# Stick-breaking weights from a scan of one product, its value halves added at the branch, and four more gate columns in a 7-product unit

## The chip, the cores and the metric

The kernel runs on one core of a Trainium2 chip. The metric is the device time of one execution in microseconds. The engines are TensorE (PE, with PEld for its weight loads), VectorE (DVE), ScalarE (ACT), GpSimd (POOL) and SyncE (SP), each with an instruction stream of its own; data moves between memory and the on-chip buffer by DMA, issued from SP and POOL.

## What is computed

One block of a transformer on 1024 tokens of width 1024, in float32: a norm and an input projection, three branches (stick-breaking attention with 8 heads of 64, forgetting attention with 8 heads of 64, attention of 4 heads of 128 over 256 memory tokens), each multiplied by a gate of 1024 columns and by a matrix of its own, their sum through an output matrix, and a squared-ReLU MLP. The change touches the stick-breaking branch and the gates:

```python
def stick_breaking_attention(q, k, v):
    """A[t,s] = beta[t,s] * prod_{s<j<t}(1-beta[t,j]), strictly causal."""
    ...
        z = jnp.einsum('bhtd,bhsd->bhts', q[:, :, q0:kend], k[:, :, :kend]) * scale
        log_rem = jnp.where(strict, jax.nn.log_sigmoid(-z), 0.0)
        after = lax.cumsum(log_rem, axis=3, reverse=True) - log_rem
        w = jnp.where(strict, jnp.exp(jax.nn.log_sigmoid(z) + after), 0.0)
        outs.append(jnp.einsum('bhts,bhsd->bhtd', w, v[:, :, :kend]))
```

With beta = sigmoid(z) and rho = 1 - beta, the weight of token s is what is left of a stick behind s, less what is left at s: A[s] = L[s+1] - L[s], where L[s] is the product of rho over s, s+1, ... up to the query.

## The kernel before

**Precision.** A float32 product is made of fp32r products (a form that TensorE multiplies at full rate): each operand is split into a high and a low part, high by ScalarE (L1054), low by VectorE as the difference (L1055), and three products are summed. A *7-product unit* is a scheme for a group of four column blocks of 128 of the input projection, in which operand sums save some products: 168 matmuls of 512 columns (or as many in pairs of 256) where four plain blocks take 4 x 48 = 192. The units are sbk, sbq, mq, fxk, fxq, sbv, ga, gb, gc, in this order (`PROJ`), the last three for the gates 16 to 19, 20 to 23 and 0 to 3 (`GATES`). The remaining gates are plain blocks (L1144).

**The order of the work.** The kernel is written as many small processes in Python that run when the program is built. Each asks a planner for operations (`Op(engine, estimated time, function, due)`), for buffers (`Get(pool)`) and for events. The planner keeps a clock per engine and takes the earliest due ready operation; a dense product is a side task, taken on TensorE only when no other TensorE operation is ready at that moment of its plan. What comes out is a fixed instruction order per engine; at run time nothing is reordered, and an engine waits at the head of its stream. Dense products are taken in one order (`dense`, L1107): values, one gate, the 7-product units, the plain gates, then the memory branch, the stick-breaking branch and, after attention, the forgetting branch.

**Attention.** `units` (L976) starts a `unit` (L887) per pair of heads, head and group of 256 queries, first the four stick-breaking pairs, then the four forgetting pairs. A unit has two tiles of 128 queries (`sb_tile` L812, `fox_tile` L851). For stick-breaking a chunk of up to 512 scores is made by two matmuls (L823, L824) into a PSUM bank; on the diagonal block VectorE adds the mask (L834); ScalarE makes two sigmoids, rho and beta (L827, L828); VectorE scans backwards (L843), c[s] = rho[s] c[s+1] + beta[s], in which c is what has been taken. The values were differenced once (`value_step` L1566) so that the product with c gives the sum over A. Then per block of 256 keys: four transposes on TensorE (*turn*, L917) into one of two TR banks, the high part by ScalarE (L922), the low part by VectorE (L924, `ptl`), four matmuls with the values (L934). At the end of a unit the result stands in PSUM as two halves of 64 rows, which ScalarE and VectorE add (L962, L963) before SP stores it to `o_scr`. Forgetting attention stores its two halves to `o_scr` and `low_scr`, and they are added when the branch fetches them (L1666, L1668). Memory attention (L627 on, normalised at L662) runs beside the last stick-breaking pairs.

**Buffers and the branches.** Three tiles of 1024 columns named `r` (pool `RR`) carry what the branches fetch; two of them are used as four half tiles for rho (`RQ`) until the stick-breaking pairs are over. `fetched_o` (L1658) loads a row block of 128 rows of a branch's attention result, `bring` (L1680) splits it into high and low parts for the matmul, and `dense_branch` (L1732) multiplies: the blocks ks[0], ks[1] first for both halves, then ks[2], ks[3]. For the stick-breaking branch, ks[2] and ks[3] are split into buffers that the memory branch reads until it is done.

## Time and profile before

| | |
|---|---|
| runs | 1685.86 us median of 3, 1685.47 to 1686.56 |
| the profiled execution | span 1686.7 us, 0.8 above that median |
| TensorE | 1675.3 us busy (99%), 9118 matmuls |
| VectorE | 1293.0 us (77%) |
| ScalarE | 848.9 us (50%) |
| POOL | 255.2 us (15%) |
| stick-breaking scores | from 483 to 703 us |
| forgetting scores | from 706 to 862 us |
| stick-breaking branch | 883 to 927 us |

The profile follows one execution. A row of the timeline is start, duration, engine, line, operation, output and inputs by the program's names, and in brackets how long the engine stood idle before it and what it waited for. A row of grouped instructions ends in the count, the busy time, the mean of one in ns, and the idle time before them. Matmuls overlap, so that their price is the distance between two starts. The granted clock is TensorE's clock as a share of the full one.

### The profile page before, as it was taken

To read this page: it belongs to the slowest core of one execution; us is meant where nothing else is said; L and a number is where in the kernel's file an instruction comes from. 1 tells how busy PE (TensorE), PEld (TensorE's weight loads), DVE (VectorE), ACT (ScalarE), POOL (GpSimd) and SP (SyncE) were. 2 spreads that over 40 slices of the span, in tenths; PEclk is the share of its full clock that TensorE was granted. 3 is DMA by queue.
4 is the path that set the end of the run, shared out by engine and by line. 5 is a ranking of instruction groups with operands and counts; after the bars stand their busy time and mean duration, and the time that the engine had idled before them with its cause. 6 is when DMAs were issued, how large, how long until landed. Compare 5 with 4: busy or idle time off the path is not lost.

```text
span 1686.7 us, 25003 instructions
## 1 busy us (share of the span) xinstructions
PE 1675.3 (99%) x9118; PEld 1432.0 (85%) x9118; DVE 1293.0 (77%) x2079; ACT 848.9 (50%) x1474; POOL 255.2 (15%) x440
## 2 busy tenths in 40 slices
PE   9999999999999999999999999999999999999999
PEld 9998899998888888888888887878888887888887
DVE  7977778855459888867877898987777776688775
ACT  6455555534358888866761446433333344332331
POOL 0000000000253151254400011022111120000000
PEclk9999999999999999999999999999999999999999
DMA  7445434467475365387747542144444484564532
GB/s 245 157 150 182 149 119 150 146 194 243 127 232 161 111 186 151 117 240 224 236 146 245 183 162 100 57 162 155 152 150 137 150 307 171 202 202 143 198 125 75
DMA packets 142221, 284.32 MB, mean 169 GB/s; under 512 B 16913, under 2 KB 53329, under 8 KB 142098
## 3 DMA queue, kind: packets, MB, share of 16 engines
q1 hardware_dynamic: 110562, 183.08, 32.0%
q0 software_dynamic: 31536, 99.64, 19.5%
q8 instruction: 72, 1.18, 0.3%
q14 instruction: 51, 0.42, 0.1%
HBM read 189.83 MB, written 92.83 MB: 168 GB/s over the span
## 4 chain that ended last, share of the span: by engine, by line
PE 92%; DVE 5%; DMA 2%; ACT 1%; issue 1%; SPq 0%; DVEq 0%; ACTq 0%
PE pp L1456 11%; PE pp L1144 10%; PE pp L1981 10%; PE pp L2658 8%; PE sc L1456 7%; PE sc L1144 6%; PE sc L1981 5%; PE sc L2658 4%; PE tr L2658 4%; PE tr L917 4%; PE pv L1456 3%; PE pv L2658 3%; PE tr L1981 2%; PE sc L934 2%; PE pp L934 2%; DVE h L1917 1%
## 5 line engine op out<-in xcount | busy, mean ns | idle before, releaser
L1055 DVE TENSOR_TENSOR wlo<-raw,whi 128x1024 fp32r<-128x1024 f32 (+1 forms) x88 | 107.5, 1222 | 80.2 <-ACT whi L1054 80.0
L1054 ACT ACTIVATE whi<-raw 128x1024 fp32r<-128x1024 f32 (+1 forms) x88 | 93.2, 1059 | 78.8 <-PE pp L1456 32.7
L2658 PE MATMUL pp<-h,sop 128*128 128x512 f32 x540 | 128.4, 396 | 0.0
L2658 PEld LDWEIGHTS pp<-h,sop 128*128 128x128 f32 x540 | 101.6, 188 | 24.4
L1981 PE MATMUL pp<-h,oh 128*128 128x512 f32 x384 | 121.1, 397 | 0.7 <-ACT cu L2066 0.6
L924 DVE TENSOR_TENSOR ptl<-tr,pth 128x512 fp32r<-128x512 f32 (+1 forms) x160 | 99.1, 628 | 24.1 <-ACT pth L922 23.1
L922 ACT ACTIVATE pth<-tr 128x512 fp32r<-128x512 f32 (+1 forms) x160 | 87.4, 556 | 36.0 <-PE sc L934 15.8
L1981 PEld LDWEIGHTS pp<-h,oh 128*128 128x128 f32 x384 | 72.0, 188 | 19.0 <-ACT cu L2066 1.4
L2573 ACT ACTIVATE h<-t 128x2048 fp32r<-128x2048 f32 (+1 forms) x17 | 30.7, 1814 | 110.2 <-DVE t L1917 97.4
L1373 POOL DMA_DIRECT2D raw<-w_in x32 | 24.2, 755 | 395.1 <-DVE wlo L1055 395.1
L1144 PE MATMUL sc<-h,whi 128*128 128x512 f32 (+1 forms) x254 | 77.7, 389 | 0.0
L1456 PE MATMUL pp<-h,whi 128*128 128x512 f32 x248 | 77.5, 394 | 0.0
L1981 PE MATMUL pp<-h,ol 128*128 128x512 f32 x192 | 76.1, 396 | 0.0
L1456 PE MATMUL pp<-whi,h 128*128 128x256 f32 x384 | 71.8, 283 | 0.0
L843 DVE TENSOR_TENSOR_SCAN e<-r,e 128x384 f32<-128x384 f32 (+3 forms) x64 | 66.3, 1044 | 6.9 <-ACT e L828 6.5
L1974 ACT ACTIVATE oh<-raw 128x512 fp32r<-128x512 f32 x64 | 39.4, 625 | 61.8 <-DVE raw L1917 61.8
L2658 PE MATMUL sc<-h,sop 128*128 128x512 f32 x264 | 63.7, 396 | 0.0
L2658 PE MATMUL tr<-h,sop 128*128 128x512 f32 x264 | 63.4, 396 | 0.0
L1917 DVE TENSOR_TENSOR sop<-ur,sop 128x2048 fp32r<-128x2048 f32 (+1 forms) x28 | 61.8, 2211 | 2.0 <-ACT sop L2586 2.0
L917 PE MATMUL tr<-ident,e 128*128 128x128 f32 x416 | 62.7, 273 | 0.0
L1456 PEld LDWEIGHTS pp<-whi,h 128*128 128x128 f32 x384 | 60.2, 188 | 0.0
L2658 PEld LDWEIGHTS sc<-h,sop 128*128 128x128 f32 x264 | 49.6, 188 | 12.3 <-DVE sop L1917 0.5
(558 smaller groups left out, 5087.7 us busy)
## 6 DMA issues: line engine op xcount, KB each, us to landing
ur<-s_scr SPq DMA_DIRECT2D x26, 1024.0 KB
raw<-w_in POOLq DMA_DIRECT2D x42, 512.0 KB, 4.9
raw<-w_up SPq DMA_DIRECT2D x60, 256.0 KB
s_scr<-s POOLq DMA_DIRECT2D x60, 256.0 KB, 2.7
g<-w_down SPq DMA_DIRECT2D x14, 1024.0 KB
s_scr<-cu POOLq DMA_DIRECT2D x48, 256.0 KB, 2.8
h<-sbk_scr POOLq DMA_DIRECT2D x64, 128.0 KB, 3.2
o<-gate_scr SPq DMA_DIRECT2D x32, 256.0 KB
```

Of the source, the lines that this page charges most:

```text
L843: nc.vector.tensor_tensor_scan(out=back, data0=rho[:, :u][:, ::-1], data1=back, initial=0.0 if last else beta[:, c + u:c + u + 1], op0=ALU ...
L917: nc.tensor.transpose(tr[:, jj * 256 + a * P:jj * 256 + (a + 1) * P], es[a][:, j * P:(j + 1) * P], ident)
L922: yield Op("ACT", act_time(512 - lo_c), lambda: nc.scalar.activation(ph[:, lo_c:], tr[:, lo_c:], AF.Copy))
L924: yield Op("DVE", dve_time(512 - lo_c), lambda: nc.vector.tensor_tensor(pl[:, lo_c:], tr[:, lo_c:], f32(ph[:, lo_c:]), ALU.subtract))
L934: nc.tensor.matmul(pv[0][:, c_:256], pair.v[:, j, b, :], p_[:, jj * 256 + c_:(jj + 1) * 256], start=(k == 0 and n_ == 0 and i == 0), stop= ...
L1054: yield Op("ACT", 0.03 + act_time(m), lambda: nc.scalar.activation(hi, raw, AF.Copy))
L1055: yield Op("DVE", dve_time(m), lambda: nc.vector.tensor_tensor(lo, raw, f32(hi), ALU.subtract))
L1144: nc.tensor.matmul(ps, a_, b_, start=(first and i == 0), stop=(last and i == n - 1))
L1456: nc.tensor.matmul(out_, a_, b_, start=(first and n == 0 and j == 0), stop=(last and n == 3 and j == len(todo) - 1), skip_group_check=True)
L1917: nc.vector.tensor_tensor(out_, a_, b_, op)
L1981: nc.tensor.matmul(ps, w[a_][:, k * P:(k + 1) * P], h[b_][k], start=(first and k == 0 and i == 0), stop=(last and k == 3 and i == 2), skip ...
L2658: nc.tensor.matmul(ps, a_[:, c, qs], b_[:, c, :], start=(kind in ("P1", "P2", "P7") and c == 0 and i == 0), stop=(kind in ("P2", "P4", "P3 ...
```

## The change

- **The scan.** L[s] = rho[s] L[s+1], from 1: the scan multiplies by rho and adds a zero. One sigmoid per score; beta, the second buffer for it and the pool `RQ` go, and the three `r` tiles are free from the start.
- **The mask.** In place of VectorE's add on the scores, POOL sets the masked entries of rho to 1 (`affine_select` on the diagonal 128 x 128 block), between the sigmoid and the scan.
- **The values** are differenced with the other sign, and 1 is subtracted from L as the blocks are read back from PSUM: ScalarE's copy gets a bias of -1 from a column `minus`, VectorE's subtraction becomes one instruction that adds -1 and subtracts the high part.
- **The halves.** A stick-breaking unit stores both halves as they are, as a forgetting unit does (`low_scr` becomes two). The branch fetches both for each row block, into two `r` tiles, and VectorE adds them.
- **The gates** 4 to 7 become a fourth gate unit `gd` of 7 products, after gc. Six plain gates stay (10 to 15), where there were ten.

```diff
-    def sb_tile(pair, b, i, beta):
+    def sb_tile(pair, b, i, left):
...
         def chunk(ci, c, m, u):
-            rho = yield Get(RQ)
             sc = yield Get(SC)
+            part = left[:, c:c + u]
...
-            def sigmoids():
-                nc.scalar.activation(rho[:, :u], sc[:, :u], AF.Sigmoid, scale=HD ** -0.5)
-                nc.scalar.activation(beta[:, c:c + u], sc[:, :u], AF.Sigmoid, scale=-HD ** -0.5)
-
             yield Op("PE", 2 * mm_time(max(m, 256)), scores)
+            yield Op("ACT", act_time(u), lambda: nc.scalar.activation(
+                part, sc[:, :u], AF.Sigmoid, scale=HD ** -0.5), table=AF.Sigmoid)
+            SC.put(sc)
             last = c + u == n
             if last:
-                dg = sc[:, u - P:u]
-                yield Op("DVE", 0.22, lambda: nc.vector.tensor_tensor(
-                    dg, dg, holder["later"][:, 385:513], ALU.add))
-            yield Op("ACT", act_time(u, u), sigmoids, table=AF.Sigmoid)
-            SC.put(sc)
-            if not last:
+                dg = left[:, n - P:n]
+                yield Op("POOL", 0.3, lambda: nc.gpsimd.affine_select(
+                    out=dg, in_=dg, pattern=[[-1, P]], compare_op=ALU.is_ge, fill=1.0, base=-1, channel_multiplier=1))
+            else:
                 yield scanned
-
-            def scan():
-                back = beta[:, c:c + u][:, ::-1]
-                nc.vector.tensor_tensor_scan(out=back, data0=rho[:, :u][:, ::-1], data1=back,
-                                             initial=0.0 if last else beta[:, c + u:c + u + 1],
-                                             op0=ALU.mult, op1=ALU.add)
-            yield Op("DVE", 0.1 + 0.00215 * u, scan, 0.14)
-            RQ.put(rho)
+            back = part[:, ::-1]
+            yield Op("DVE", 0.1 + 0.00215 * u, lambda: nc.vector.tensor_tensor_scan(
+                out=back, data0=back, data1=zero.to_broadcast([P, u]),
+                initial=1.0 if last else left[:, c + u:c + u + 1], op0=ALU.mult, op1=ALU.add), 0.14)
...
-            yield Op("ACT", act_time(512 - lo_c), lambda: nc.scalar.activation(ph[:, lo_c:], tr[:, lo_c:], AF.Copy))
+            h_, t_ = ph[:, lo_c:], tr[:, lo_c:]
+            yield Op("ACT", act_time(512 - lo_c), lambda: nc.scalar.activation(
+                h_, t_, AF.Identity, bias=minus) if of_sb else nc.scalar.activation(h_, t_, AF.Copy))
             pl = yield Get(PL)
-            yield Op("DVE", dve_time(512 - lo_c), lambda: nc.vector.tensor_tensor(
-                pl[:, lo_c:], tr[:, lo_c:], f32(ph[:, lo_c:]), ALU.subtract))
+            yield Op("DVE", dve_time(512 - lo_c), lambda: nc.vector.scalar_tensor_tensor(
+                pl[:, lo_c:], t_, -1.0, f32(h_), ALU.add, ALU.subtract) if of_sb else nc.vector.tensor_tensor(
+                pl[:, lo_c:], t_, f32(h_), ALU.subtract))
...
-        if pair.kind == "fox":
...
-        else:
-            o = ob[:HD, :]
-            yield Op("ACT", act_time(256), lambda: nc.scalar.activation(o, pv[0][HD:P, :256], AF.Copy))
-            yield Op("DVE", dve_time(256), lambda: nc.vector.tensor_tensor(o, o, pv[0][0:HD, :256], ALU.add))
-            PV.put(pv[0])
-            yield Op("SP", 0.1, lambda: nc.sync.dma_start(scr[rows, cols], o), 2.5)
+        yield Op("ACT", act_time(256), lambda: nc.scalar.activation(ob, pv[0][:, :256], AF.Copy))
+        PV.put(pv[0])
+
+        def halves():
+            nc.sync.dma_start(scr[rows, cols], ob[:HD, :])
+            nc.sync.dma_start(low[rows, cols], ob[HD:, :])
+        yield Op("SP", 0.2, halves, 3.0)
...
-    GATES = {"ga": 16, "gb": 20, "gc": 0}
+    GATES = {"ga": 16, "gb": 20, "gc": 0, "gd": 4}
...
-        yield Op("DVE", dve_time(512), lambda: nc.vector.tensor_tensor(a, a, b, ALU.subtract))
+        yield Op("DVE", dve_time(512), lambda: nc.vector.tensor_tensor(a, b, a, ALU.subtract))
...
-        halves = [RR.free.popleft() for _ in range(2)]
-        RQ.put(*(t[:, i * 512:(i + 1) * 512] for t in halves for i in range(2)))
-        spawn(whole_again(halves))
...
     def fetched_o(bi, k):
 
-        raw_ = yield Get(RR)
+        raw_, *low_ = (yield Get(RR, 2)) if bi == 1 else [(yield Get(RR))]
         raw, rows = raw_[:, :S], slice(k * P, (k + 1) * P)
         yield from transfer(lambda: nc.sync.dma_start(raw, o_scr[order[bi][1]][rows, :]), P * S * 4)
+        if bi == 1:
+            t = low_[0]
+            yield from transfer(lambda: nc.sync.dma_start(t, low_scr[0][rows, :]), P * S * 4)
+            yield Op("DVE", dve_time(S), lambda: nc.vector.tensor_tensor(raw, raw, t, ALU.add))
+            RR.put(t)
         if bi == 2:
             t = yield Get(RR)
-            yield from transfer(lambda: nc.sync.dma_start(t, low_scr[rows, :]), P * S * 4)
+            yield from transfer(lambda: nc.sync.dma_start(t, low_scr[1][rows, :]), P * S * 4)
```

Since the planner sets the order, the change moves instructions on every engine. In the pieces below the lines are those of the program they come from: the dense product is L1144 before and L1134 after, a turn L917 and L911, a product with values L934 and L931, the scores of stick-breaking L823, L824 and L824, L825. `g` and `h` are tiles of tokens or of attention results, `whi`/`wlo` high and low parts of weights, `pth`/`ptl` the two parts of a turned block, `e`/`es` rows of weights before they are turned, `sc`, `pp`, `pv`, `tr` PSUM banks.

First TensorE late in stick-breaking, with a plain gate between the pieces of attention, before:

```order
L934 MATMUL sc_137<-ptl_4802,v_4689 128x256
L1144 MATMUL pp_134<-g_122,whi_167 128x512
L1144 MATMUL pp_134<-g_126,whi_167 128x512
L1144 MATMUL pp_134<-g_122,wlo_168 128x512
L823 MATMUL pp_133<-h_4684,h_4682 128x512
L824 MATMUL pp_133<-h_4686,h_4682 128x512
L1144 MATMUL pp_134<-g_123,whi_167 128x512
L1144 MATMUL pp_134<-g_127,whi_167 128x512
L1144 MATMUL pp_134<-g_123,wlo_168 128x512
L934 MATMUL sc_137<-pth_4799,v_4689 128x256
```

And after, at the end of the last plain gate:

```order
L1134 MATMUL sc_139<-g_125,whi_169 128x512
L1134 MATMUL sc_139<-g_129,whi_169 128x512
L1134 MATMUL sc_139<-g_125,wlo_170 128x512
L824 MATMUL sc_138<-h_4899,h_4907 128x384
L825 MATMUL sc_138<-h_4905,h_4907 128x384
L911 MATMUL tr_140<-ident,e_4912 128x128
L911 MATMUL tr_140<-ident,e_4913 128x128
L911 MATMUL tr_140<-ident,e_4912 128x128
L911 MATMUL tr_140<-ident,e_4913 128x128
L931 MATMUL pp_137<-pth_5018,v_4908 128x256
L931 MATMUL pp_137<-ptl_5020,v_4908 128x256
```

Behind this point the next dense matmul stands 593 rows further on, the first of the memory branch; between them are attention and memory attention alone.

VectorE beside it after, a little into that piece (L920 is the low part of a stick-breaking block, L838 the scan, L661 and L663 the normalisation of memory attention):

```order
L920 SCALAR_TENSOR_TENSOR ptl_5020<-tr_140,pth_5018 128x512
L920 SCALAR_TENSOR_TENSOR ptl_5021<-tr_141,pth_5019 128x384
L661 RECIPROCAL st_6531<-st_6531 128x4
L663 TENSOR_SCALAR r_4914<-r_4914,st_6531 128x256 x4
L838 SCALAR_TENSOR_TENSOR e_4910<-e_4910,sm 128x384
L920 SCALAR_TENSOR_TENSOR ptl_5020<-tr_140,pth_5018 128x512
L920 SCALAR_TENSOR_TENSOR ptl_5021<-tr_141,pth_5019 128x512
L838 SCALAR_TENSOR_TENSOR e_4910<-e_4910,sm 128x512
L838 SCALAR_TENSOR_TENSOR e_4911<-e_4911,sm 128x512
```

No mask add stands between them any more, and the scan reads one row of weights in place of two.

Next VectorE between the memory branch and the stick-breaking branch, before (L1779 and L1781 evict results of a branch, L1055 is the low part of a split):

```order
L1779 TENSOR_TENSOR g_7469<-pp_134,o_4811 128x512
L1055 TENSOR_TENSOR wlo_164<-r_4694,whi_163 128x512
L1055 TENSOR_TENSOR h_7212<-r_4695,h_7212 128x512
L1055 TENSOR_TENSOR h_7213<-r_4696,h_7213 128x512
L1055 TENSOR_TENSOR wlo_164<-r_4694,whi_163 128x512
L1055 TENSOR_TENSOR h_7212<-r_4695,h_7212 128x512
L1055 TENSOR_TENSOR h_7213<-r_4696,h_7213 128x512
```

And after (L1649 adds the halves of a stick-breaking block, L1655 those of a forgetting block, L1766 and L1768 evict, L1045 is the low part of a split):

```order
L1649 TENSOR_TENSOR r_4914<-r_4914,r_4915 128x1024
L613 RECIPROCAL fn<-fn 128x16
L1766 TENSOR_TENSOR g_6608<-sc_139,o_5030 128x512
L1045 TENSOR_TENSOR wlo_168<-r_4914,whi_167 128x512
L1045 TENSOR_TENSOR h_6344<-r_4916,h_6344 128x512
L1045 TENSOR_TENSOR wlo_168<-r_4914,whi_167 128x512
L1045 TENSOR_TENSOR h_6344<-r_4916,h_6344 128x512
L1045 TENSOR_TENSOR wlo_170<-raw_171,whi_169 128x1024
L1649 TENSOR_TENSOR r_4915<-r_4915,r_4914 128x1024
L1045 TENSOR_TENSOR h_6343<-r_4915,h_6343 128x512 x2
L1655 TENSOR_TENSOR r_4916<-r_4916,e_4911 128x1024
```

Three tiles that held three fetched blocks now hold one block with its low half, and the next block's low half goes into the tile that the first leaves. SP's queue there, after (L1645 loads `o_scr`, L1648 the low half of a stick-breaking block, L1653 that of a forgetting block):

```order
L1645 DMA r_4915<-o_scr_75 128x1024
L1645 DMA r_4916<-o_scr_76 128x1024
L1645 DMA e_4910<-o_scr_76 128x1024
L1648 DMA r_4914<-low_scr_78 128x1024
L1653 DMA e_4911<-low_scr_79 128x1024
```

The low half of the last stick-breaking block stands behind two loads of the forgetting branch. TensorE's matmuls of that branch, after:

```order
L1134 MATMUL pp_135<-whi_167,whi_165 128x512
L1134 MATMUL pp_135<-wlo_168,whi_165 128x512
L1134 MATMUL pp_135<-whi_167,wlo_166 128x512
L1134 MATMUL pp_135<-h_6343,whi_165 128x512 x2
L1134 MATMUL pp_135<-h_6343,wlo_166 128x512
```

`h_6343` is the last block, reached after 15 matmuls of the branch.

26 lines of the change are left out of this document (9 added, 17 removed).

## Prediction

> **What bounds the kernel now.** I read first the page's engine totals and the shares of its chain:
>
> ```profile
> span 1686.7 us, 25003 instructions
> PE 1675.3 (99%) x9118; PEld 1432.0 (85%) x9118; DVE 1293.0 (77%) x2079; ACT 848.9 (50%) x1474; POOL 255.2 (15%) x440
> PE 92%; DVE 5%; DMA 2%; ACT 1%; issue 1%; SPq 0%; DVEq 0%; ACTq 0%
> ```
>
> TensorE is busy 99% of the span and holds 92% of the chain. So the time is the sum of its matmuls plus the moments in which it has none. An edit to VectorE, ScalarE or POOL counts only where TensorE waits for them. Next, the windows by stage (columns: stretch, length, PE, PEld, DVE, ACT, POOL busy, granted clock, DMA share, GB/s): dense products before attention, stick-breaking, forgetting attention, the second branch's product.
>
> ```profile
> 60.00:489.00 429.00, 428.77 (x2746) 387.99 (x2745) 296.47 (x494) 205.99 (x320) 43.80 (x68) 1.00 0.52 164
> 489.00:708.00 219.00, 219.00 (x1364) 193.29 (x1364) 191.16 (x343) 188.84 (x420) 68.53 (x123) 1.00 0.54 158
> 708.00:882.00 174.00, 172.53 (x1101) 152.17 (x1100) 133.65 (x358) 122.42 (x278) 63.51 (x117) 0.99 0.67 201
> 882.00:927.00 45.00, 45.00 (x197) 36.46 (x196) 35.02 (x48) 8.87 (x12) 2.24 (x3) 1.00 0.76 244
> ```
>
> In the stick-breaking stage TensorE is busy for 219.00 of 219.00 us although VectorE works 191 and ScalarE 189: dense gate matmuls between the attention matmuls keep it fed. The only place in attention where it runs dry is at 740, found in the list of waits and then on the timelines and windows:
>
> ```profile
> 731.58 0.33 SPq L1663 DMA_DIRECT2D r<-o_scr  x1
> 740.50 0.63 ACT L1054 ACTIVATE h<-r 128x512 fp32r<-128x512 f32 x1 [3.58 <-DMA r<-o_scr]
> 742.59 0.50 PE L869 MATMUL pv<-h,h 128*128 128x512 f32 x1 [1.47 <-DVE st L874]
> 740.33:743.75 3.42, 1.95 (x9) 1.14 (x8) 2.58 (x9) 3.04 (x6) 0.00 (x0) 1.00 0.96 322
> 743.75:747.16 3.41, 3.41 (x10) 2.61 (x9) 1.22 (x8) 2.05 (x4) 0.00 (x0) 0.50 0.99 342
> 1023.60:1027.00 3.40, 1.86 (x14) 1.59 (x14) 3.26 (x9) 3.33 (x6) 0.00 (x0) 1.00 0.94 280
> ```
>
> A 512 KB load took 8.9 us from issue to its reader (731.58 to 740.50), TensorE stood 1.47 us, and the next 3.41 us ran at a granted clock of 0.50, which loses about 1.7 us more. A like shortfall at 1023.60 shows 1.00 in its own window.
>
> **Matmuls.** Gates 4 to 7 took 4 x 48 = 192 matmuls of 512 columns; as a fourth 7-product unit they take 168.
>
> ```profile
> 160.82 5.57 PE pp L1456 x24
> 784.84 0.62 PE L917 MATMUL tr<-ident,e 128*128 128x128 f32 x4
> 785.22 0.42 PE L869 MATMUL pv<-h,h 128*128 128x384 f32 x1
> 785.48 0.34 PE L870 MATMUL pv<-h,h 68*128 68x384 f32 x1
> 785.65 0.28 PE L934 MATMUL pp<-pth,v 128*128 128x256 f32 x1
> 785.77 0.28 PE L934 MATMUL pp<-ptl,v 128*128 128x256 f32 x1
> ```
>
> 24 in 5.57 us is 0.232 each; 24 fewer save 5.6 us. The scores, turns and products stay. The unit's operand sums, splits and evictions lie in the stage 60 to 489, where VectorE has 132 us free and ScalarE 223: taken at nothing; without that cover they would cost their own time. Start to start, 128 columns cost 0.095 (four turns, 784.84 to 785.22), 256 cost 0.12, 384 cost 0.17.
>
> **The stretch without dense work.** With six dense gates left instead of ten, their matmuls run out in the order before stick-breaking ends. From the last of them to the first matmul of the memory branch there now stand 96 matmuls of 512 columns, 20 of 384, 226 of 256 and 287 of 128, attention and memory attention alone: 22.3 + 3.4 + 27.1 + 27.3 = 80 us of TensorE with nothing to fill it. The longest such piece before was about 5 us, and in it lies the stall at 740. What VectorE has to do beside those 80 us, by the rows of before:
>
> ```profile
> L843 DVE TENSOR_TENSOR_SCAN e<-r,e 128x512 f32<-128x512 f32 x40 | 50.4, 1264 | 3.5 <-ACT e L828 3.1
> L843 DVE TENSOR_TENSOR_SCAN e<-r,e 128x384 f32<-128x384 f32 x8 | 7.5, 943 | 1.9 <-ACT e L828 1.9
> L924 DVE TENSOR_TENSOR ptl<-tr,pth 128x512 fp32r<-128x512 f32 x96 | 65.1, 682 | 18.4 <-ACT pth L922 17.7 <-PE pp L824 0.3
> L924 DVE TENSOR_TENSOR ptl<-tr,pth 128x384 fp32r<-128x384 f32 x64 | 35.0, 546 | 5.7 <-ACT pth L922 5.4
> L874 DVE CUSTOM_DVE_ANT_0 e<-pv,sm 128x512 f32<-128x512 f32 x31 | 21.3, 687 | 6.6 <-PE pv L870 6.3
> L662 DVE TENSOR_SCALAR r<-r,st 128x256 f32<-128x256 f32 x32 | 9.8, 369 | 0.3
> L739 DVE SCALAR_TENSOR_TENSOR sn<-tr,sm,sn 128x512 fp32r<-128x512 f32 x26 | 19.1, 745 | 4.2 <-ACT sn L738 4.2
> 737.08 0.68 DVE L924 TENSOR_TENSOR ptl<-tr,pth 128x512 fp32r<-128x512 f32 x1
> 737.68 0.68 DVE L874 CUSTOM_DVE_ANT_0 e<-pv,sm 128x512 f32<-128x512 f32 x1
> ```
>
> Its first 53 instructions there (12 scans of 512, 4 of 384, 6 shorter; 13 low halves of 512, 8 of 384; 4 normalisations; one split of 1024; two maxima; three tiny ones) sum to 39.1 us by these durations, and back to back they start 0.60 apart where one lasts 0.68, so 0.08 overlaps: 39.1 - 53 x 0.08 = 34.9. TensorE's part between the same turns is 27.7: VectorE is 7.2 us short and cannot be ahead by more than two blocks (two TR banks), about 1.2 us. The other 152 instructions sum to 62.7 - 12.1 = 50.6 against 52.1 of TensorE, so nothing is won back. To this come VectorE's own waits for ScalarE's half of each block: 18.4/96 = 0.19 for 512 columns and 5.7/64 = 0.09 for 384; with 29 and 20 blocks, 7.4 us. Sum 14.6: I take **+15**. Floor 6 (7.2 less the lead); ceiling 29 (no overlap at all: 101.8 - 79.8 = 22, and the waits). The halves of stick-breaking with the -1 are a form that before has from PSUM only at 745 (L739) where I use 682; 25 of them would add 1.6, inside the range.
>
> Small idles spread over 100 us may halve the clock now and then, as behind 740: I take one such case, **+2**, floor none, ceiling three (5). By the Trainium skill, TensorE: Matmul & The Clock Gate, Part 1, the clock drops only after an idle window of about 3.4 us; the row at 740.33, half idle with 1.95 busy and then 0.50, speaks against it, and the one at 1023.60 for it. By that rule the sum would be 2 us less.
>
> **The seam between the memory and the stick-breaking branch.** Before, the last two row blocks of the second branch (each 512 KB, at line 1663) had been fetched at 842 to 856, in three tiles, and only had to be split: no wait at 882. Now each also needs its low half, so a second tile, a second load and an add; for the last block the tiles come free only when the block ahead is added and split. Count from E, the end of the memory branch's last matmul. The block ahead is split into a weight buffer that this branch reads until E, and VectorE's last eviction stands in front: 0.69 and four splits 0.61 apart, ScalarE's 0.63 beside them, end at E + 3.1. SP's queue has two transfers of the third branch ahead of the low half, one of them waiting for the same splits, so with two issues of 0.44 ahead it goes at about E + 4. How long such a load takes:
>
> ```profile
> 842.09 0.44 SPq L1663 DMA_DIRECT2D r<-o_scr  x1
> 846.18 0.63 ACT L1054 ACTIVATE h<-r 128x512 fp32r<-128x512 f32 x1 [0.68 <-DMA r<-o_scr]
> 884.31 0.42 SPq L1666 DMA_DIRECT2D r<-low_scr  x1
> 890.78 1.22 DVE L1668 TENSOR_TENSOR r<-r,r 128x1024 f32<-128x1024 f32 x1
> 741.17 0.69 DVE L1055 TENSOR_TENSOR h<-r,h 128x512 fp32r<-128x512 f32 x1 [2.32 <-ACT h L1054]
> ```
>
> 4.1 us at 842, at most 6.5 at 884, 8.9 at 731. I take 6.5, the one at the same kind of place (a low half at the end of a branch); then the add 1.22, the half on ScalarE 0.63 and the other on VectorE 0.69: ready at E + 13. TensorE has 15 matmuls of other blocks, 3.5 us, and would stand for **9.6** us (7.2 with a load of 4.1; 12.0 with 8.9). So long a stall is followed by half clock as at 743.75, **+2**. By the Trainium skill, DMA: Bandwidth & Descriptors, Anatomy of one DMA, a load of this size would take some 3.2 us, an estimate from its fit; no run here is as quick, and by it the sum would be 3 less.
>
> **What is taken at nothing.**
>
> ```profile
> L834 DVE TENSOR_TENSOR pv<-pv,later 128x128 f32<-128x128 f32 x38 | 10.9, 287 | 3.9 <-PE pv L824 3.7
> L827 ACT ACTIVATE r<-pp 128x512 f32<-128x512 f32 x29 | 17.7, 609 | 3.8 <-DVE pp L834 2.5 <-PE pp L824 0.8 <-DVE pv L834 0.4
> L963 DVE TENSOR_TENSOR ob<-ob,sc 64x256 f32<-64x256 f32 x18 | 7.2, 400 | 2.0 <-ACT ob L962 1.9
> L1563 POOL TENSOR_SCALAR_AFFINE_SELECT later<-later 128x129 f32<-128x129 f32 x1 | 0.3, 293 | 0.1
> L1004 POOL DMA_DIRECT2D h<-sbk_scr x64 | 33.3, 527 | 97.1 <-PE pv L151 29.6 <-DVE wlo L1055 19.1 <-PE pp L824 13.2
> ```
>
> The 64 mask adds (0.287) and 32 halves' adds (0.40) leave VectorE, 31 us; the 96 second sigmoids (up to 0.61) leave ScalarE. TensorE waited for neither at 489 to 708, so they give nothing back there; what they give in the bare stretch is in its count above. POOL gets 64 selects at 0.29. A select that stands behind a pair's loads (0.53 each, several in a row) delays one scan by up to some 4 us; while dense matmuls fill in, that costs nothing, in the bare stretch it is a rival's price. The scan keeps its operation, so I keep its 1264. The stall at 740 (1.5 + 1.7) may go or come again inside the stretch: no term, 3 each way in the range. The 32 more half stores and the 4 more loads are issued by SP, beside TensorE; only the last counts, above.
>
> Sum on the profiled execution: 1686.7 - 5.6 + 15 + 2 + 9.6 + 2 = 1709.7. That execution's span stood 0.8 above the median of the runs, so the forecast is **1709**.
>
> **Rivals.** (1) More is lost than counted: the selects on POOL queue behind loads while nothing fills in, or the clock halves again and again. Eight pair loads of stick-breaking precede; two selects late by 4 us each, three more clock halvings (5) and the ceiling of 29: 1709 + 8 + 5 + 14 = 1736, so 1723 to 1740, chance 0.14. For it: nothing covers the stretch. Against it: most pairs are loaded before. (2) VectorE keeps up, only the seam costs: its instructions overlap by 0.22 rather than 0.08 (11.4/53, what the first part needs), and the stretch costs under 2: 1686.7 - 5.6 + 2 + 9.6 + 2 - 0.8 = 1694, with a 4.1 load 1691; 1688 to 1695 in all, chance 0.14. Against it: the two rows at 737. (3) **The other side**: TensorE never starves. The one point that decides is VectorE's real pace back to back. If it gains 0.22 an instruction or more, the stretch is free, the stall at 740 goes (-3.2), and the seam's chain of six VectorE steps shrinks by 1.3; with a load of 4.1 it leaves 5.9, unclocked: 1686.7 - 5.6 - 3.2 + 5.9 - 0.8 = 1683, and with the low half issued before E's splits 1677. Chance of under 1682.5: 0.06; of 1682.5 to 1688: 0.06. Against it: before, 5 us without dense work were enough to run dry. (4) That the change does not do what it says: the order shows fewer sigmoids, no mask add and 24 fewer matmuls, so no chance of its own.
>
> **The numbers.** My case, 1695 to 1723, has 0.60 (on 1685.9: from -5.6 + 6 + 0 + 7.2 + 2 to -5.6 + 25 + 4 + 12 + 2), rival 1 has 0.14, rival 2 0.14, rival 3 with its border 0.12. Leaving out the upper half of rival 1 and rival 3: range 1688 to 1728. A measurement of this kernel tells about 0.2% (3.4 us) from no change, so 1682.5 to 1689.2 counts as the same: 0.06 and a part of rival 2, 0.02, is 0.08. Faster 0.06, slower 0.86.
>
> **What would show it.** In the profile after: 9094 matmuls; TensorE busy visibly under 100% in the windows of the last third of stick-breaking and the start of forgetting attention, its waits there ending on VectorE (halves, scans, maxima); one stall of about 10 us in the dense branch product, ended by a chain from the load of the low half; granted clock under 1 right behind it. I would be wrong if the bare stretch shows TensorE busy throughout, if the last low half lands before its 15 covering matmuls end, or if a stall appears in the fourth gate unit.

## The result and the profile after

The changed kernel takes 1738.83 us in the median of 4 runs (1736.94 to 1742.8), the kernel before 1686.16 beside it: ratio 1.0316, interval 1.0302 to 1.0331. It is slower by 53 us where 23 were forecast, and lies outside the range. The profiled execution has a span of 1735.2, 48.5 above that of before (it is the quickest of the four, so that it has 4 us less to explain than the medians). The page's span, engine totals and shares of the chain:

```profile
span 1735.2 us, 24982 instructions
PE 1689.4 (97%) x9094; PEld 1434.2 (83%) x9094; DVE 1286.7 (74%) x2001; ACT 816.5 (47%) x1379; POOL 285.0 (16%) x504
PE 83%; DVE 7%; DMA 4%; issue 3%; ACT 2%; POOL 1%; SPq 0%; POOLq 0%; ACTq 0%; DVEq 0%
```

24 matmuls fewer, as meant; yet TensorE's share of the chain has fallen from 92 to 83%. VectorE, DMA, ScalarE and POOL now hold time that was TensorE's. The windows say where (columns as before): stick-breaking up to the last plain gate, the stretch without dense work in its two parts, one stop in it and what follows, the stop in the stick-breaking branch and the half clock behind it, and the half clock behind a later stop.

```profile
489.00:663.00 174.00, 171.72 (x991) 147.70 (x990) 118.12 (x159) 103.84 (x203) 85.99 (x160) 1.00 0.57 172
674.98:716.40 41.42, 31.32 (x209) 25.84 (x208) 35.36 (x53) 30.36 (x61) 21.19 (x41) 1.00 0.51 153
716.40:793.17 76.77, 64.20 (x424) 55.11 (x422) 54.57 (x152) 53.70 (x136) 33.28 (x63) 0.97 0.54 161
712.90:716.00 3.10, 0.03 (x1) 0.00 (x0) 3.10 (x6) 2.04 (x7) 1.71 (x4) 1.00 0.82 246
716.00:719.40 3.40, 3.38 (x17) 3.38 (x18) 1.26 (x2) 0.80 (x2) 0.00 (x0) 0.53 0.74 268
913.60:923.50 9.90, 0.22 (x1) 0.00 (x0) 2.21 (x2) 0.61 (x2) 0.75 (x1) 0.70 0.95 356
923.57:927.86 4.29, 4.29 (x9) 3.09 (x10) 4.29 (x6) 0.47 (x1) 0.00 (x0) 0.50 0.29 109
1071.22:1074.63 3.41, 3.41 (x13) 2.90 (x12) 2.90 (x5) 3.41 (x8) 0.00 (x0) 0.50 0.69 263
```

The two parts of the stretch without dense work (the bare stretch) took 41.4 and 76.8 us for matmuls worth 27.7 and 52.1: 118.2 for 79.6 us, 38.6 lost. (By the trace, the matmuls before 716.40 are worth 26.6, so the split is good to 1 us.) For 22.7 of the 38.6 TensorE stands; in the rest it counts as busy, but its matmuls start further apart than in a dense piece, 2.5 us of that by two pieces of half clock, from 716.23 and from 791.33. In the second part no engine is busy for more than 64 of 77 us. The waits between 660 and 810, for TensorE, VectorE and ScalarE (total, times, longest), go round in a ring:

```profile
PE tr L911 <- DVE ptl L921: 7.0, 6, 2.3
PE tr L911 <- DVE ptl L920: 6.1, 4, 3.1
...
DVE ptl L921 <- ACT pth L918: 9.0, 10, 1.5
DVE ptl L920 <- ACT pth L917: 6.4, 7, 1.7
...
ACT pth L917 <- PE pp L931: 6.7, 6, 2.5
```

TensorE waits for VectorE's low part, VectorE for ScalarE's high part, ScalarE for TensorE's product. What holds the ring up differs from stop to stop. The chain of work (its view names engine, tile and line) through the longest stop, 3.09 us, and then ScalarE and VectorE ahead of the second longest, 2.29 us:

```profile
712.86 1.14 DVE es L838
714.00 0.32 DVE es L867
714.32 1.20 DVE e L838
715.52 0.46 DVE ptl L920
716.02 0.96 PE tr L911 x4
```

```profile
789.61 0.63 ACT L1044 ACTIVATE whi<-r 128x512 fp32r<-128x512 f32 x1 [1.53 <-DMA r<-o_scr]
790.15 0.58 ACT L918 ACTIVATE pth<-tr 128x512 fp32r<-128x512 f32 x1
790.88 0.68 DVE L921 TENSOR_TENSOR ptl<-tr,pth 128x512 fp32r<-128x512 f32 x1
```

In the first, VectorE never stood: scans (L838) and a maximum of forgetting attention (L867) came before the low part in its stream. In the second, ScalarE stood for a load of the branch, and the high part came behind it. The seam, on the timelines of SP, VectorE, ScalarE and TensorE:

```profile
914.23 0.42 SPq L1648 DMA_DIRECT2D r<-low_scr  x1
921.63 1.23 DVE L1649 TENSOR_TENSOR r<-r,r 128x1024 f32<-128x1024 f32 x1 [7.05 <-DMA r<-low_scr]
922.89 1.15 ACT L1044 ACTIVATE h<-r 128x512 fp32r<-128x512 f32 x2 [9.57 <-DVE r L1649]
923.57 0.79 PE L1134 MATMUL pp<-h,whi 128*128 128x512 f32 x1 [9.75 <-ACT h L1044]
```

The low half of the last block reaches its reader 7.4 us after its issue, the add and the split follow, and TensorE has stood 9.75 us.

The account of the 48.5 us: matmuls -5.6; bare stretch +38.6; stop at the seam 9.75 and half clock behind it 2.1 (0.50 over 4.29 us), +11.9; waits on the selects at 546 to 570, +2.3 (shown below); the old stall at 740 no longer there, -3.2; the stop behind attention, 2.59 at 1067.96 with half clock behind it where before has 1.54 at 1023.62 and full clock, +2.8. That is 46.8; the rest was not followed. Attention takes some 3% more than these prices under cover too (before, 489 to 663: 174.0 us for matmuls worth 168.7), so that some 2.5 of the 38.6 are no loss of cover.

### The profile page after: what moved, and what is told of

Its sections match the earlier page's. It is cut to its first block, busy times and chain, and to the rows that moved or that the text cites. A ratio compares the mean times of both kernels' runs of the same rounds, so it can differ in the third digit from the quotient of the medians.

```text
span 1735.2 us, 24982 instructions
## 1 busy us (share of the span) xinstructions
PE 1689.4 (97%) x9094; PEld 1434.2 (83%) x9094; DVE 1286.7 (74%) x2001; ACT 816.5 (47%) x1379; POOL 285.0 (16%) x504
## 4 chain that ended last, share of the span: by engine, by line
PE 83%; DVE 7%; DMA 4%; issue 3%; ACT 2%; POOL 1%; SPq 0%; POOLq 0%; ACTq 0%; DVEq 0%
PE pp L1446 11%; PE pp L1968 10%; PE pp L2645 8%; PE sc L1446 7%; PE pp L1134 7%; PE sc L1968 5%; PE sc L2645 4%; PE tr L2645 4%; PE sc L1134 4%; PE pv L1446 3%; PE tr L911 3%; PE pv L2645 3%; PE tr L1968 2%; PE pp L931 2%; DMA raw<-w_in 2%
## 5 line engine op out<-in xcount | busy, mean ns | idle before, releaser
L1045 DVE TENSOR_TENSOR wlo<-raw,whi 128x1024 fp32r<-128x1024 f32 (+1 forms) x90 | 110.1, 1223 | 108.2 <-ACT whi L1044 108.0
L1446 PE MATMUL pp<-h,whi 128*128 128x512 f32 x296 | 92.7, 394 | 0.0
L838 DVE TENSOR_TENSOR_SCAN e<-e,sm 128x512 f32<-128x512 f32 (+3 forms) x64 | 65.8, 1050 | 10.3 <-POOL e L833 9.8
L911 PE MATMUL tr<-ident,e 128*128 128x128 f32 x416 | 63.3, 277 | 9.0 <-DVE ptl L920 5.8
L1134 PE MATMUL pp<-h,whi 128*128 128x512 f32 x192 | 62.0, 403 | 9.8 <-ACT h L1044 9.8
L1446 PEld LDWEIGHTS pp<-h,whi 128*128 128x128 f32 x296 | 55.6, 188 | 12.9
L911 PEld LDWEIGHTS tr<-ident,e 128*128 128x128 f32 x416 | 49.1, 142 | 18.6 <-DVE ptl L920 6.1
L921 DVE TENSOR_TENSOR ptl<-tr,pth 128x512 fp32r<-128x512 f32 (+1 forms) x80 | 49.8, 633 | 19.1 <-ACT pth L918 18.9
L920 DVE SCALAR_TENSOR_TENSOR ptl<-tr,pth 128x384 fp32r<-128x384 f32 (+1 forms) x80 | 49.0, 625 | 18.5 <-ACT pth L917 18.3
```

What stands on the lines that cost most here:

```text
L838: yield Op("DVE", 0.1 + 0.00215 * u, lambda: nc.vector.tensor_tensor_scan(out=back, data0=back, data1=zero.to_broadcast([P, u]), initial=1 ...
L911: nc.tensor.transpose(tr[:, jj * 256 + a * P:jj * 256 + (a + 1) * P], es[a][:, j * P:(j + 1) * P], ident)
L920: yield Op("DVE", dve_time(512 - lo_c), lambda: nc.vector.scalar_tensor_tensor(pl[:, lo_c:], t_, -1.0, f32(h_), ALU.add, ALU.subtract) if ...
L921: pl[:, lo_c:], t_, -1.0, f32(h_), ALU.add, ALU.subtract) if of_sb else nc.vector.tensor_tensor(
L1045: yield Op("DVE", dve_time(m), lambda: nc.vector.tensor_tensor(lo, raw, f32(hi), ALU.subtract))
L1134: nc.tensor.matmul(ps, a_, b_, start=(first and i == 0), stop=(last and i == n - 1))
```

## The experiments

The theory at the start (A): the loss in the stretch is a lack of dense work. The rivals: the stick-breaking chain itself became slower (B, through the selects on POOL or the new forms), and for the seam, that another load ends last there (C). All edits are to the changed kernel unless it says so.

**Dense work put back that nothing needs**, in the changed kernel and, as a control, in the one before:

```diff
     gates = [dense_gate(n, may_gate) for n in (*range(16, 24), *range(0, 8), *range(10, 14)) ...]
+    gates += [dense_gate(n, may_gate) for n in range(10, 14)]
```

> The changed kernel with the plain gates 10 to 13 made a second time, behind the others in the dense order and with the same result: 192 matmuls of 512 columns, 44.5 us of TensorE work that nothing needs, and what ScalarE, VectorE and SP do for them. The longest bare stretch falls from 79.6 to 4.3 us. Theory A (the 38.8 us lost in the bare stretch are a lack of dense work, so the same work put there costs nothing): 1738.8 + 44.5 - 38.8 + 0 = 1745, 1738 to 1752. Rival (the stretch loses its time for reasons that dense work would not cover): 1783, 1772 or more.

> The same four gates a second time in the kernel before, where attention had its dense work already. Theory A: they find no idle TensorE and cost their price, 1685.9 + 44.5 = 1730, perhaps less 3 for the stall at 740, 1725 to 1733. Rival: below 1715.

1746.66 us (1744.54 to 1747.97) against 1738.83: 44.5 us of useless matmuls cost 8. In the kernel before the same cost 43.5: 1729.72 against 1686.25. The first kernel's windows, the stretch and the seam:

```profile
660.00:800.00 140.00, 139.86 (x886) 123.35 (x885) 101.45 (x218) 101.01 (x230) 60.88 (x115) 1.00 0.58 180
905.00:950.00 45.00, 34.75 (x168) 27.85 (x168) 28.92 (x40) 13.40 (x24) 1.50 (x2) 0.89 0.63 210
```

TensorE is busy for 139.86 of 140 us where it had starved, with the same attention, selects and forms; only the seam is left. This is the clearest run of the study: the lost time was empty, and dense work fills it.

**The two halves of the change in the gates.** The changed kernel without the fourth unit, and the kernel before with nothing else:

```diff
-    GATES = {"ga": 16, "gb": 20, "gc": 0, "gd": 4}
+    GATES = {"ga": 16, "gb": 20, "gc": 0}
```

> The changed kernel without the fourth gate unit: gates 4 to 7 are plain dense products again, all else of the change stays. The longest piece of attention without dense work on TensorE falls from 79.6 to 4.3 us of matmuls. Theory A (the loss in the bare stretch, 38 us, comes from the missing dense work): it goes, 5.6 us of matmuls come back, the wait between the branches (12 us with its half clock) stays: 1738.8 - 38 - 3 + 5.6 = 1703, at most 1707, at least 1697. Rival B (the stick-breaking chain itself became slower, by the selects on POOL or by the new forms on VectorE): at least 25 us of the loss stay, 1725 or more.

> The kernel before with nothing but the fourth gate unit; arithmetic, mask, sigmoids and halves of stick-breaking as before. A piece of 74.2 us of attention matmuls has no dense work in it. Theory A: it costs as much per us as in the changed kernel (38.6 lost on 79.6, 0.48 each), 36 us, less 5.6 of matmuls and the old stall at 740 (3): 1686.2 + 27 = 1713, between 1705 and 1722. Rival B: the unit saves its 5.6 us, and the old chain, with the mask on VectorE, loses little: 1680 to 1688.

1709.78 us (ratio 1.0143, 1.0128 to 1.0158), 3 above A's range and far under B's mark, and 1720.10 (1.0209, 1.0192 to 1.0226), inside A's range. The first in two windows of its own, the second over its bare stretch:

```profile
660.00:800.00 140.00, 139.85 (x895) 123.84 (x895) 105.51 (x263) 100.86 (x235) 61.52 (x115) 1.00 0.68 208
500.00:540.00 40.00, 37.17 (x230) 32.13 (x230) 27.93 (x37) 23.80 (x45) 24.32 (x45) 1.00 0.71 198
```

```profile
666.73:779.07 112.34, 91.51 (x596) 75.20 (x595) 96.34 (x213) 91.88 (x218) 40.94 (x77) 0.98 0.45 139
```

With ten plain gates the stretch is full again. What stays is the seam, in that order 12.6 us of standing instead of 9.75, and 2.8 at 500 to 540: 7 more than expected. The fourth unit alone, in the old arithmetic, costs 34.5: it saves 5.6 and loses 38.1 on 74.2 us. So the loss is not of the new scan's making.

**The selects on POOL**, turned to a tile that nobody reads, in the same order:

```diff
-                    out=dg, in_=dg, pattern=[[-1, P]], ...
+                    out=aside, in_=aside, pattern=[[-1, 32]], ...
```

> The changed kernel with every select on POOL turned to a small tile of its own of 32 columns, so that no scan waits for POOL; the order on TensorE, VectorE and ScalarE stays the same. The mask is left out, so the stick-breaking weights are those without it. Theory A: the selects are not the cause; the waits that name POOL in the bare stretch are 2.8 us: 1733 to 1739. Rival B (selects late behind pair loads make the loss): half of it or more goes, below 1722.

1730.70 us, 8 less, 2 beyond what A allowed; the profiled spans differ by 5.0. The windows of its bare stretch and of the place ahead:

```profile
670.96:788.98 118.02, 95.70 (x631) 81.25 (x630) 89.49 (x204) 83.63 (x198) 49.01 (x96) 0.97 0.52 157
500.00:600.00 100.00, 100.00 (x566) 86.07 (x565) 64.29 (x84) 56.12 (x109) 51.99 (x111) 1.00 0.63 196
```

The stretch takes 118.0 us, as before; TensorE's 2.3 us of waits between 489 and 663 are gone. Rival B holds ahead of the stretch, for the 2.3 us of those waits and perhaps a little more, and not for the 38.6.

**What sets the rate of the loss.** First VectorE: scans of 128 columns, then low parts of 8 columns, both in the same order.

```diff
+            back = back[:, :P]
...
-                pl[:, lo_c:], t_, -1.0, f32(h_), ALU.add, ALU.subtract)
+                pl[:, lo_c:lo_c + 8], t_[:, :8], -1.0, f32(h_)[:, :8], ALU.add, ALU.subtract)
```

> The changed kernel with every scan cut to its first 128 columns, same order on every engine; the rest of each row stays the bare sigmoid, so the weights are not those of the reference. In the bare stretch VectorE has 13 us less to do, all in its first part, which took 41.4 us for 27.7 us of matmuls. Theory A1 (VectorE's amount of work sets that part): 10 us or more of its 13.7 go: 1728 or less. Theory A2 (the round trip of a block through TensorE, ScalarE and VectorE sets it, with two blocks in flight): at most 5 go, 1734 to 1739, and the second part, 76.8 us for 52.1, stays in both.

> The changed kernel with VectorE's low part of every turned block cut to 8 columns and the high part used twice in the product with the values, so the low part is left out of the result; the order stays. In the bare stretch VectorE has 49 x 0.55 = 27 us less to do, and the step between ScalarE's half and the next turn in the same bank is some 0.1 us instead of 0.68. Theory B1 (the round trip of a block over VectorE is what TensorE waits for): at least 15 of the 38.8 go, 1724 or less. Theory B2 (TensorE waits for whatever stands at the head of the other streams, loads and stores among it, and each stop shows because nothing dense covers it): less than 8 go, 1731 or more.

1732.52 us, between the marks of A1 and A2, and 1731.65, just on the side of B2; the stretch took 113.8 and 113.5, 4 to 5 less. Of the second the whole stretch; then both parts, cut at the same turn (716.02 in the changed kernel, where they took 41.0 and 77.2), of the short scans and of the short low parts:

```profile
675.21:788.66 113.45, 96.04 (x631) 83.48 (x630) 68.65 (x203) 82.11 (x197) 55.58 (x105) 0.95 0.54 161
674.44:710.12 35.68, 30.46 (x207) 25.57 (x205) 23.46 (x52) 27.60 (x55) 17.15 (x39) 1.00 0.52 153
710.12:788.26 78.14, 63.14 (x425) 54.02 (x425) 54.69 (x151) 54.97 (x142) 35.61 (x68) 0.99 0.57 169
675.43:713.61 38.18, 31.76 (x206) 27.04 (x204) 28.31 (x52) 29.27 (x60) 21.88 (x41) 0.95 0.50 158
713.61:788.66 75.05, 64.06 (x424) 56.26 (x425) 40.27 (x151) 52.72 (x137) 33.70 (x64) 0.95 0.56 164
```

VectorE is busy for 69 of 113 us, 21 less than it was, and TensorE starves almost as much. In the second part, which holds most of the loss, the amount of VectorE's work, on which the forecast had been built, sets little: 14.7 us less of it won 2.1. In the first part it is a link, but not the only one: 11.5 us less won 5.4 there, half of what A1 asked for. The shares of the chain in that part, in the changed kernel and with the short low parts ("issue" is time in which an engine waited for nothing that the profile shows; L833 is the select, L994, L592 and L1030 are loads):

```profile
by line: DVE e L838 32.6%; issue 26.0%; DVE ptl L920 12.9%; DVE es L838 7.6%; PE tr L911 6.7%; DVE ptl L684 4.7%; PE pp L931 4.3%; ACT pth L917 3.4%; DVE wlo L1045 2.8%; PE pv L1134 1.7%; PE tr L678 1.6%; ACT pth L682 1.2%; ACT ob L949 0.9%
by line: issue 65.6%; POOL h L994 21.7%; POOL e L833 5.6%; POOL h L592 3.8%; POOL es L833 3.4%; DVE es L838 3.4%; DVE e L838 3.1%; POOL v L1030 2.4%; DVE es L867 1.5%; POOLq L833 1.0%; DVE ptl L920 0.2%; DVE st L867 0.0%
```

VectorE's scans and low parts hold most of the first chain. With less for VectorE to do, the chain lies on POOL's loads and selects, and the part is 2.9 us shorter; that POOL sets the time then was not tested. Next the depth of the ring: three tiles for the two parts of a block, three banks for the turns, and both.

```diff
-        opened("A2", (PH, "pth", 2, 512, F32R), (PL, "ptl", 2, 512, F32R), ...
+        opened("A2", (PH, "pth", 3, 512, F32R), (PL, "ptl", 3, 512, F32R), ...
...
-        for place in (PP, PP, SC, SC, PV, PV):
+        for place in (PP, TR, SC, SC, PV, PV):
```

> The changed kernel with three tiles each for the high and low parts of turned blocks in place of two, paid for with two of 19 h tiles; the PSUM banks stay two. The planner makes another order: the longest bare stretch is 45.1 us in place of 79.6, others 4 to 7. If only the length of the bare stretch counts (0.49 lost per us): 1738.8 - 38.8 + 22 = 1722. Theory A2 (two blocks in flight set the loss): less than half of that rate, 1708 to 1714. Neither: above 1732.

> The changed kernel with three PSUM banks for turned blocks during attention in place of two; the third comes from the dense products (one bank instead of two) and goes back when memory attention is over. High and low parts keep two tiles each. The longest bare stretch is 56.0 us of matmuls. If only its length counts (0.49 lost per us): 1738.8 - 38.8 + 27 = 1727, 1722 to 1732. Theory A2 (TensorE waits at the next turn for a bank that VectorE has not read, so the number of banks sets the loss): less than half of that rate, 1700 to 1714.

> Three banks for turned blocks and three tiles each for their high and low parts (two h tiles fewer). Longest bare stretches 31.1 and 8.2 us of matmuls. If only the length counts: 1738.8 - 38.8 + 0.49 x 39 = 1719, 1714 to 1724. Theory A2: at half of that rate or less, 1700 to 1710. The wait between the branches stays in both (10 to 12 us).

1729.34, 1733.79 and 1725.61 us: all above what A2 allowed, and each 7 above what the length alone would give. Their longest stretches, in that order:

```profile
704.02:773.41 69.39, 58.32 (x359) 48.34 (x358) 52.44 (x128) 52.77 (x124) 30.68 (x59) 0.94 0.57 171
```

```profile
690.26:777.19 86.93, 71.16 (x450) 60.64 (x449) 61.77 (x143) 58.37 (x140) 37.29 (x72) 0.92 0.58 176
```

```profile
709.70:763.04 53.34, 42.90 (x235) 33.77 (x234) 33.95 (x95) 32.69 (x82) 22.83 (x42) 0.90 0.60 178
```

Shorter stretches, since the planner spread the gates otherwise, but lost at the same rate or a worse one. What their longest stops wait for: with three banks and three tiles, ScalarE at the head of its stream for a tile whose store is still under way; with three banks, VectorE for a select behind POOL's loads.

```profile
719.93 0.60 ACT L702 ACTIVATE o<-pp 128x512 f32<-128x512 f32 x1 [6.34 <-DMA gate_scr<-o]
721.35 0.79 PE L1134 MATMUL pp<-pth,h 128*128 128x512 f32 x1 [5.48 <-ACT pth L682]
```

```profile
700.36 0.52 POOL L994 DMA_DIRECT2D h<-fq_scr  x1 [3.42 <-DMA raw<-w_b]
702.17 1.29 DVE L838 TENSOR_TENSOR_SCAN es<-es,sm 128x512 f32<-128x512 f32 x1 [7.23 <-POOL es L833]
704.10 1.12 PE L911 MATMUL tr<-ident,e 128*128 128x128 f32 x4 [4.58 <-DVE ptl L920]
```

Neither wait has to do with the block that TensorE waits for. Each engine takes its instructions in the program's order, so a store, a load or a select at the head of one stream stops the ring.

**The mask back on the scores**, as before the change:

```diff
-            if last:
-                dg = left[:, n - P:n]
-                yield Op("POOL", 0.3, lambda: nc.gpsimd.affine_select(...))
+                dg = sc[:, u - P:u]
+                yield Op("DVE", 0.22, lambda: nc.vector.tensor_tensor(dg, dg, holder["later"][:, 385:513], ALU.add))
```

> The changed kernel with the mask added to the scores by VectorE ahead of the sigmoid, as before the change, in place of the select on POOL. The planner makes another order, with bare stretches of 46.4, 6.7 and 4.2 us. Theory A (0.49 lost per us without dense work): 1738.8 - 38.8 + 0.49 x 53 = 1726, less 2.7 for the early waits at 546 to 570 if those are the selects': 1723, between 1718 and 1729. Rival B (64 mask adds of 0.29 back on VectorE make up for it): 1733 or more.

1722.96 us (1722.89 to 1723.03): as A said, by another order with a shorter stretch.

**Of the change only the scan**, with ten plain gates and the halves added in the unit; then the same with the mask on the scores. The edit of the halves stands further below, at the seam, that of the mask just above.

> Of the change only the scan with its one sigmoid, the select on POOL and the -1: ten plain gates, and a unit adds its halves itself as before. One bare stretch of 14.1 us of matmuls late in stick-breaking. Theory A: 0.49 x 14 = 7 lost there, 3 to 4 by early waits on the selects as in the first experiment, the old stall at 740 (3) gone or not, no wait between the branches: 1686 + 7 + 3 - 3 = 1693, 1689 to 1698. Rival B (the new chain is slower by itself): above 1700.

> As the run before, with the mask added to the scores by VectorE as it was: only the scan, the single sigmoid and the -1 are new. No bare stretch over 5.0 us of matmuls, no select on POOL, no second load per block. Theory A: nothing that TensorE waits for has changed but for the better: 1683 to 1688, the same as before within 0.2%, since VectorE and ScalarE were not what it waited for. Rival B: 1693 or more.

1708.08 us (1705.67 to 1711.17), 10 above A's range and past B's mark, and 1688.65 (ratio 1.0016, 1.0006 to 1.0025), 0.7 above A's. The first in its bare stretch:

```profile
774.62 0.63 ACT L1051 ACTIVATE whi<-r 128x512 fp32r<-128x512 f32 x1 [3.90 <-DMA r<-o_scr]
776.57 1.12 PE L911 MATMUL tr<-ident,e 128*128 128x128 f32 x4 [5.05 <-DVE ptl L921]
```

14.1 us of matmuls took 27.9 there; one load of a block, at the head of ScalarE's stream, stopped TensorE for 5 us. The second has no such stretch:

```profile
489.00:708.00 219.00, 219.00 (x1381) 193.30 (x1380) 195.60 (x367) 167.26 (x333) 73.84 (x134) 1.00 0.52 160
```

TensorE is as busy as it was before, and the time is that of before plus 0.16%: the scan, the single sigmoid and the -1 bring nothing, since nobody waited for what they save. The two kernels differ in the place of the mask alone, and in the order that the planner makes with it: 19.4 us. In the changed kernel the same step was worth 15.9 (1738.83 to 1722.96). With the selects aside and the order kept it was 8; so a good part of their price lies in the order, which has the longer bare stretch when the mask is on POOL (79.6 against 46.4 us, and 14.1 against 5.0). The second kernel here is the best version with any part of the change; none beats the kernel before.

**The seam.** The halves added in the unit, one tile and one load per block; and, with ten plain gates, the third branch's fetches held back until the last low half is in:

```diff
+            yield Op("ACT", act_time(256), lambda: nc.scalar.activation(o, pv[0][HD:P, :256], AF.Copy))
+            yield Op("DVE", dve_time(256), lambda: nc.vector.tensor_tensor(o, o, pv[0][0:HD, :256], ALU.add))
...
     def last_operands(in_O):
+        yield low_in
```

> The changed kernel, but a stick-breaking unit adds its two halves itself and stores one, as before the change, and the branch loads one tile per row block. Theory A: the stall of 9.75 us in the stick-breaking branch and the half clock behind it (2.3) go; the bare stretch is 84.8 us of matmuls in place of 79.6 (+2.5): 1738.8 - 12 + 2.5 = 1729, 1724 to 1734. Rival C (another load ends last there, and the stall only moves): 1736 or more.

> The first experiment (ten plain gates, all else of the change), and the forgetting branch's fetches wait until the last stick-breaking block and its low half have been fetched, so that all three r tiles serve that branch ahead of the seam. Theory A: the stall of 12.6 us in the stick-breaking branch and the half clock behind it go, 15 us: 1709.8 - 15 = 1695, between 1691 and 1699; what is left over before are the waits at 500 to 540 and after 1040. Rival C (the third branch's blocks now come too late, and the stall moves to its start): 1703 or more.

1733.46 us and 1703.39 (ratio 1.0103, 1.0086 to 1.0120). The first's windows of the stretch and of the branch:

```profile
669.36:803.46 134.10, 109.55 (x672) 93.15 (x671) 100.36 (x228) 95.28 (x221) 58.23 (x111) 0.91 0.49 150
885.00:935.00 50.00, 50.00 (x289) 43.01 (x289) 33.78 (x68) 24.41 (x49) 1.50 (x2) 1.00 0.51 165
```

The stop is gone, 50 of 50; the gain is 5 rather than 10, since the bare stretch, 84.8 us of matmuls in this order, lost 49. In the second the stop moved, as rival C had it, to the start of the third branch:

```profile
936.77 1.22 DVE L1664 TENSOR_TENSOR e<-e,r 128x1024 f32<-128x1024 f32 x1 [2.79 <-DMA r<-l_scr]
938.03 0.63 ACT L1044 ACTIVATE h<-e 128x512 fp32r<-128x512 f32 x1 [5.80 <-DVE e L1664]
938.71 1.22 PE L150 MATMUL sc<-h,whi 128*128 128x512 f32 x2 [4.64 <-ACT h L1044]
```

In these two orders the three tiles are too few for both branches: whichever is served first, the other's blocks come late.

All longest bare stretches, the matmuls in them by the prices of the prediction (256 columns at 0.118), the time they took and what was lost per us:

| kernel | matmuls, us | took, us | lost per us |
|---|---|---|---|
| the changed kernel | 79.6 | 118.2 | 0.48 |
| fourth unit alone | 74.2 | 112.3 | 0.51 |
| selects aside | 79.6 | 118.0 | 0.48 |
| short scans | 79.6 | 113.8 | 0.43 |
| low part of 8 columns | 79.6 | 113.5 | 0.43 |
| halves in the unit | 84.8 | 134.1 | 0.58 |
| three tiles | 45.1 | 69.4 | 0.54 |
| three banks | 56.0 | 86.9 | 0.55 |
| three of both | 31.1 | 53.3 | 0.71 |
| mask on the scores | 46.4 | 67.8 | 0.46 |
| scan alone, select on POOL | 14.1 | 27.9 | 0.98 |

## Why the prediction was wrong

- **What bounds it: right.** TensorE's matmuls and the moments without them. The direction followed from this, and so did the two main places.
- **Matmuls, -5.6: right.** 9094 of them; where nothing starves, the same kernel with and without 192 others differs by 43.5 for 44.5. The unit's sums, taken at nothing, cost nothing: TensorE is busy for 428.81 of 429 us from 60 to 489.
- **The stretch, +15, floor 6, ceiling 29: this step failed.** Place and length were right (from 674.98 to 793.17, 79.6 us of matmuls); the price was 38.6. The step counted what VectorE has to do, and found it short by 7.2 in the first part and balanced in the second ("nothing is won back"), with 7.4 of waits on ScalarE. In the first part that was the right link and the right amount, 35 us of VectorE where 34.9 were counted; the loss was 13.7. In the second part, taken as balanced, 24.7 were lost, and there the mechanism was wrong. An engine busy for 54.57 of 76.77 us does not bound by its amount: here each engine waits for another in a ring, in fixed order, and with no dense work between, what holds up any of them reaches TensorE. With 21 us of VectorE's work cut away, 33.9 of the 38.6 stayed. The ceiling of 29 looked like a bound and was none: it let VectorE work through the stretch without a break but for the 7.4, and VectorE was busy for 89.9 of 118.2 us; its waits for ScalarE's half alone came to 15.4 between 660 and 810. Before has only one such piece, of 5 us; with 3.2 us lost on it, it gives 0.6 per us, and 0.6 of 80 would have been 50: too much, but nearer than 15, and it was not used.
- **The seam, 9.6 and 2: right.** 9.75 and 2.1; the low half was taken at 6.5 us and took 7.4, issued at 914.23, by a queue as described. By the Trainium skill, DMA: Bandwidth & Descriptors, Anatomy of one DMA, such a load would be some 3.2 us (an estimate from its fit, which is given there for loads that GpSimd issues; these are SP's); the traces have 4.1 to 8.9 ahead and 7.4 here, with the DMA share at 0.95 in that window.
- **Half clock in the stretch, +2: about right.** Two pieces where one was taken, at 716.23 and 791.33; what lies in the stretch cost 2.5.
- **The selects, taken at nothing: wrong.** 2.3 us of waits, ahead of the bare stretch and not in it, where they had been feared; 8 in the medians with the order kept; and 16 with the order that the planner makes without them. That the mask's place changes the order, and with it how long the dense work lasts, was not priced by itself.
- **Rivals.** Rival 1 named nearly the time (1736) by luck: its ceiling for the stretch was passed by 10, and its late selects and further clock halvings (8 and 5) came to 2.3 and 3.4. Rival 2 and the other side fell, each for the same reason as the forecast's size: they also reckoned with VectorE's pace.
- **What stays open.** Why the rate is near 0.5 in pieces of 45 to 85 us. VectorE's amount, the scans, the selects, the tiles and the banks each do not set it alone; when one is eased, another stands close behind. ScalarE's steps and the exact order of the streams were not varied by themselves.

## What to carry to other kernels

Work that can run at any time is worth most where the critical engine has nothing else, so a cheaper way of doing it that moves it forward in time can cost more than it saves: here 5.6 us of matmuls were saved and 44.5 us of cover moved out of attention. Before such a move, list in the new order the longest piece without cover, and price it by how the critical engine fares in uncovered pieces of the old trace, not by another engine's busy time. To test it, put useless work of the same size into the place: if the time hardly changes, the place was empty.

## What the runs showed of the hardware

- A stop of 1.5 to 3 us can halve the granted clock: 3.09 us of standing at 712.93 were followed by 0.53 over 3.40 us, 2.29 at 789.33 by 0.50, and 1.47 us in the kernel before by 0.50. By the Trainium skill, TensorE: Matmul & The Clock Gate, Part 1, it takes an idle window of about 3.4 us; these three rows have less. But its length alone does not decide: 2.18 us at 865.56 in the kernel with the scan alone and the select on POOL, and 2.11 at 1044.52 with ten plain gates, were followed by 1.00, and from 674.98 to 712.93 the clock stayed at 1.00 with 7 of 38 us idle in stops of 0.2 to 1.6 us.
- One load of 512 KB from SP's queue took between 4.1 and 9.3 us from issue to its reader in these traces, and the time went up, roughly, with the busy share of the DMA engines meanwhile: 4.1 us at 0.68 (842.09, before), 6.2 at 0.88 (902.26), 7.4 at 0.94 (914.23), 8.9 at 1.05 (731.58, before), 9.3 at 0.98 (887.85, with ten plain gates). Other loads of the size ahead of it in the queue are not needed for that: the one at 731.58 had none within 8 us.
